# The up projection of a two-layer trunk's MLP by Strassen's seven products, with the tokens' operands made once a layer

## The chip, the core and the metric

The kernel runs on one core of one Trainium2 chip, with nothing on the other cores. Its metric is the device time of one execution in microseconds (us). Before the change three runs gave 2859.17 us (median), 2856.69 us (lowest) and 2861.38 us (highest).

## What is computed

1024 tokens of 1024 features pass a decoder trunk of two layers in float32: an HGRN2 mixer and an MLP, then latent attention (MLA) and a second MLP, then a last norm. The change lies in the two MLPs, which are alike:

```
def rmsnorm(x, gain):
    y = xf * lax.rsqrt(jnp.mean(xf * xf, axis=-1, keepdims=True) + EPS)
    return (y * gain).astype(x.dtype)

def sq_relu_mlp(xn, w_up, w_down):              # 1024 -> 4096 -> 1024 features
    return jnp.square(jax.nn.relu(xn @ w_up)) @ w_down

for l in range(DEPTH):
    h = h + mixer(rmsnorm(h, ...))              # HGRN2 for l = 0, MLA for l = 1
    h = h + sq_relu_mlp(rmsnorm(h, mlp_norm[l]), mlp_w_up[l], mlp_w_down[l])
return rmsnorm(h, final_norm)
```

## The kernel before

Features lie on the 128 partitions and tokens along the rows. The residual stream is two tiles `res` (the code's `hT[0]`, `hT[1]`), one for each half of 512 tokens, eight blocks of 128 features in each. Every product is made to nearly full float32 precision from three matmuls: an operand is split into a high part (a ScalarE cast) and a low part (the operand less its high part, on VectorE or GpSimd), and high x high, high x low and low x high are added up in PSUM (`mm3`, L92 to L98). A matmul here always moves 512 columns.

The stages follow each other: HGRN2 (0 to about 650 us), first MLP (to about 1350), MLA (to about 2165), second MLP (to about 2848), and the end.

An MLP of before begins with the norm. `inv_rms` squares eight blocks on ScalarE (L472), adds them on VectorE (L474), sums over the partitions with one matmul by ones (L476), and makes 1/rms by Ln, Exp and one Newton step (L478 to L480, L108 to L110). `fnorm` makes each normed block (L490) and `split` its parts (L90 on ScalarE, L91 on VectorE), 512 columns at a time, into the tiles `xn`. This is done for the first half of the tokens under a high priority, and for the second half between the first hidden features. Its temporary tiles come from a pool (`npers`, seven tiles) that all stages share.

Then come 4096 hidden features. `hidden` (L519) makes 128 of them for 512 tokens by 24 matmuls (L98) and squares the ReLU (L529, L530). The first and the last 256 of them go by `plain`: 96 matmuls up and 96 down, all L98. The other 3584 go by seven blocks of `fast`, 512 hidden features each: 192 matmuls up (L98), then the down product by Winograd's form of Strassen's scheme, seven products of 24 matmuls each (L613), over halves of the hidden features, of the outputs and of the tokens. Sums of weights are made on GpSimd and sums of hidden features on VectorE (L595), the parts by L600 and L601 (weights) and L90, L91 (`hh`, `hl`), with three buffers for each of `hh` and `hl`. Each product's four PSUM tiles are added to the stream by VectorE (L618).

A scheduler sets the order of each engine's instructions when the program is built, by program order and priority; at run time each engine works through its own list in order and waits on semaphores. A tile can be written only when whoever used that piece of memory before is through.

## Time and profile before

| | |
|---|---|
| median of 3 runs | 2859.17 us |
| span of the profiled execution | 2859.5 us |
| PE (TensorE matmul) busy | 2741.5 us, 96% |
| DVE (VectorE) busy | 1783.7 us, 62% |
| POOL (GpSimd) busy | 1054.6 us, 37% |
| ACT (ScalarE) busy | 896.9 us, 31% |
| matmuls L98 and L613 on the chain that ended last | 45% and 19% of the span |

Engine names in the profile: PE is TensorE's matmul, PEld its weight load, DVE is VectorE, ACT is ScalarE, POOL is GpSimd, SP is the queue that issues DMAs. The record of a matmul is longer (about 390 ns) than its share of the pipeline, so the cost of a matmul is read from the chain of waits, where a piece is a stretch of matmuls with its count. "a <- b" beside a wait names the instruction that ended it. PEclk is the granted TensorE clock as a share of full speed (2.4 GHz); 0.5 is its lower level (1.2 GHz).

### The profile page before, as it was taken

How to read it: one execution, taken by the hardware profiler on the slowest of the kernel's cores; microseconds unless marked ns; L12 is line 12 of the kernel's file. 1: busy time of each engine (PE TensorE's matmuls, PEld its weight loads, DVE VectorE, ACT ScalarE, POOL GpSimd, SP SyncE). 2: the span in 40 equal slices, each digit the busy share in tenths (PEclk: the TensorE clock that was granted, in tenths of full speed). 3: DMA queues.
4: the chain of work that ended last, by engine and by line, in shares of the span. 5: the costliest groups of instructions: out<-in, count | busy, mean ns of one | idle time of the engine just before them, and what ended most of it. 6: DMA issues, size and time to landing. Idle time of an engine off the chain costs nothing.

```text
span 2859.5 us, 34588 instructions
## 1 busy us (share of the span) xinstructions
PE 2741.5 (96%) x13573; PEld 2271.3 (79%) x13573; DVE 1783.7 (62%) x2924; ACT 896.9 (31%) x1672; POOL 1054.6 (37%) x584
## 2 busy tenths in 40 slices
PE   7999999898999999999889999999999999999998
PEld 5877777677888888887678888888887888888886
DVE  6667767766455566546676666676668455556555
ACT  4222233222222222222354444444445222222223
POOL 3222223343445455444321223122222455455443
PEclk9999999899999999999999999999999999999999
DMA  4111112133111111101211111111101111111102
GB/s 128 37 38 38 30 38 60 59 92 96 37 45 52 59 59 59 52 23 42 66 44 34 28 47 37 40 29 50 45 22 67 40 42 54 57 59 60 52 23 74
DMA packets 149665, 143.95 MB, mean 50 GB/s; under 512 B 11458, under 2 KB 122111, under 8 KB 149503
## 3 DMA queue, kind: packets, MB, share of 16 engines
q1 hardware_dynamic: 149502, 141.75, 16.4%
q8 instruction: 107, 1.75, 0.3%
q14 instruction: 56, 0.45, 0.1%
HBM read 133.33 MB, written 4.19 MB: 48 GB/s over the span
## 4 chain that ended last, share of the span: by engine, by line
PE 82%; DVE 12%; ACT 3%; issue 2%; DMA 0%; POOL 0%; SPq 0%; DVEq 0%; ACTq 0%; POOLq 0%
PE mm L98 45%; PE dn L613 19%; PE s L856 6%; PE nb L889 3%; PE mm L896 2%; PE x L356 2%; PE dn L98 2%; DVE xn L91 1%; DVE y L110 1%; ACT P L862 1%; DVE acc L474 1%; DVE t L109 1%; PE x L253 1%; DVE k L332 1%; DVE t L108 1%
## 5 line engine op out<-in xcount | busy, mean ns | idle before, releaser
L98 PE MATMUL mm<-xn,wh 128*128 128x512 f32 x3776 | 1206.2, 397 | 12.9 <-DVE res L435 8.0
L98 PEld LDWEIGHTS mm<-xn,wh 128*128 128x128 f32 x3776 | 708.2, 190 | 157.7 <-issue 11.0
L98 PE MATMUL mm<-xn,wl 128*128 128x512 f32 x1888 | 748.0, 396 | 0.0
L136 POOL TENSOR_TENSOR wl<-wst,wh 128x1024 fp32r<-128x1024 f32 (+2 forms) x165 | 394.9, 2396 | 250.0 <-ACT wh L133 241.6
L98 PEld LDWEIGHTS mm<-xn,wl 128*128 128x128 f32 x1888 | 358.0, 190 | 72.0 <-issue 1.1
L135 POOL TENSOR_SCALAR wh<-wst 128x1024 fp32r<-128x1024 f32 (+2 forms) x129 | 142.7, 1109 | 344.0 <-PE mm L98 218.9
L529 ACT ACTIVATE r<-mm 128x512 f32<-128x512 f32 x128 | 76.2, 595 | 582.2 <-PE mm L98 582.1
L618 DVE TENSOR_TENSOR res<-res,dn 128x512 f32<-128x512 f32 x308 | 201.5, 680 | 70.3 <-PE dn L613 69.1
L601 POOL TENSOR_TENSOR wl<-wa,wh 128x1024 fp32r<-128x1024 f32 x56 | 134.6, 2404 | 267.1 <-ACT wh L600 267.1
L865 POOL TENSOR_SCALAR P<-P,rc 128x128 f32<-128x128 f32 (+1 forms) x64 | 52.2, 815 | 347.9 <-DVE rc L863 333.5
L601 POOL TENSOR_TENSOR wl<-ws,wh 128x1024 fp32r<-128x1024 f32 x42 | 100.9, 2403 | 202.5 <-ACT wh L600 202.5
L613 PE MATMUL dn<-hh,wh 128*128 128x512 f32 x392 | 153.2, 391 | 0.0
L613 PE MATMUL dn<-wh,hh 128*128 128x512 f32 x392 | 153.2, 391 | 0.0
L613 PE MATMUL dn<-wh,hl 128*128 128x512 f32 x392 | 152.7, 389 | 0.0
L613 PE MATMUL dn<-hl,wh 128*128 128x512 f32 x392 | 152.7, 389 | 0.0
L613 PE MATMUL dn<-wl,hh 128*128 128x512 f32 x392 | 152.7, 389 | 0.0
L613 PE MATMUL dn<-hh,wl 128*128 128x512 f32 x392 | 152.7, 389 | 0.0
L530 DVE TENSOR_TENSOR fr<-r,mm 128x512 f32<-128x512 f32 x56 | 37.8, 685 | 175.8 <-ACT r L529 175.3
L530 DVE TENSOR_TENSOR res<-r,mm 128x512 f32<-128x512 f32 x56 | 37.8, 685 | 175.8 <-ACT r L529 175.4
L91 DVE TENSOR_TENSOR hl<-bs,hh 128x1024 fp32r<-128x1024 f32 x42 | 104.5, 2489 | 60.4 <-ACT hh L90 60.4
L862 ACT ACTIVATE P<-s,mx 128x384 f32<-128x384 f32 (+7 forms) x128 | 95.0, 743 | 138.0 <-DVE mx L860 118.2
L889 PE MATMUL nb<-h,xn 128*128 128x256 f32 (+1 forms) x640 | 136.7, 292 | 0.1
(253 smaller groups left out, 5213.2 us busy)
## 6 DMA issues: line engine op xcount, KB each, us to landing
wst<-mlp_w_up SPq DMA_DIRECT2D x64, 512.0 KB, 3.7
wa<-mlp_w_down SPq DMA_DIRECT2D x56, 512.0 KB, 3.8
wst<-hgrn_w_o SPq DMA_DIRECT2D x16, 512.0 KB, 3.7
wst<-mla_w_o SPq DMA_DIRECT2D x16, 512.0 KB, 3.7
wst<-hgrn_w_q SPq DMA_DIRECT2D x10, 512.0 KB, 3.8
wst<-hgrn_w_i SPq DMA_DIRECT2D x10, 512.0 KB, 3.7
wst<-hgrn_w_g SPq DMA_DIRECT2D x10, 512.0 KB, 3.7
wst<-hgrn_w_f SPq DMA_DIRECT2D x9, 512.0 KB, 3.7
```

Source lines behind the costliest of these rows:

```text
L91: V.tensor_tensor(out=out_l, in0=src, in1=out_h.bitcast(F32), op=ALU.subtract)
L98: T.matmul(ps, l, r, start=i == 0, stop=i == n - 1)
L135: G.tensor_scalar(out=wh[:, cs], in0=st[:, cs], scalar1=1.0, scalar2=1.0, op0=ALU.mult, op1=ALU.mult)
L136: G.tensor_tensor(out=wl[:, cs], in0=st[:, cs], in1=wh[:, cs].bitcast(F32), op=ALU.subtract)
L529: S.activation(out=r, in_=ps, func=AF.Relu)
L530: V.tensor_tensor(out=f, in0=r, in1=ps, op=ALU.mult)
L601: G.tensor_tensor(out=wl, in0=wa, in1=wh.bitcast(F32), op=ALU.subtract)
L613: T.matmul(banks[i], l, r, start=start and n == 0, stop=n == 5, skip_group_check=not start)
L618: V.tensor_tensor(out=o, in0=o, in1=banks[i], op=ALU.add)
L856: T.matmul(ps[:, at + u * HALF:at + u * HALF + w_], l, r, start=e == 0, stop=e == len(terms) - 1)
L862: S.activation(out=pt[:, :n], in_=sc, func=AF.Exp, bias=mx, accum_out=sm)
L889: T.matmul(dst, l, r[:, cols_], start=j == 0 and e == 0, stop=j == 2 * g + 1 and e == 2)
```

## The change

The up projection goes by the same seven-product scheme, for 256 hidden features at a time: over halves of the hidden features, of the input features and of the tokens. A product is 12 matmuls (L608), so 256 features take 84 matmuls; before they took four tiles of 24, which is 96. The down projection goes by `fast`'s scheme for all eight blocks of 512 features (`times`, L692; VectorE's add is L699), and `plain` is gone. In the whole program 13067 matmuls become 12635: 432 fewer, 216 in each layer (192 up, 24 down).

The token side of the up products are seven operands, made once a layer, each with a high and a low part: the two quarters B11, B21 and B22 of the normed tokens as they are, and the sums T1 to T4. `inverse` makes 1/rms for both halves of the tokens, with one tile each for the sum and the square; `normed` makes the normed quarters as float32 (L561); `rest` makes the second half, the sums (`combine`) and all remaining parts (`halves`, L567 and L525), 1024 columns at a time. `rest` stands behind the first two products in the first `up`. T1 needs the second half of the tokens; T2 and T3 need the sums too.

The temporary tiles of `inverse` are now the MLP stage's own tiles `hh` and `hl` (two buffers each, three before), and the pools for weights, norm and PSUM belong to a stage (`common`) instead of the whole program. Weights are loaded and split 512 columns at a time: five raw buffers, four pairs of parts.

```
-            NB = DFF // 256
-            def hidden(up, j, u, f):
-                mm3(ps, [(up[k // 4][0][:, k % 4, js], up[k // 4][1][:, k % 4, js], xh[:, k, :], xl[:, k, :])
-                         for k in range(KT)])
...
+            def inverse(u):
+                ta, tb = wide(tag="hh"), wide(F32, tag="hl")
+                acc, s, y, t = ta[:, 0], ta[:, 1], tb[:, 0], tb[:, 1]
+                for k in range(KT):
+                    sq = acc if k == 0 else s
+                    S.activation(out=sq, in_=hT[u][:, k, :], func=AF.Square)
+                    if k:
+                        V.tensor_tensor(out=acc, in0=acc, in1=sq, op=ALU.add)
+                ps = pbank()
+                T.matmul(ps, onef, acc, start=True, stop=True)
...
+            def halves(eng, key, src):
+                for k in (slice(0, 2), slice(2, 4)):
+                    S.copy(out=X[key][0][:, k], in_=src[:, k])
+                    sub(eng, X[key][1][:, k], src[:, k], X[key][0][:, k].bitcast(F32))
...
+            def rest():
+                normed(0, 1, y1)
+                combine(V, f[0, 1], f[0, 1], f[0, 0])
+                normed(1, 1, y1)
+                halves(G, "B22", f[1, 1])
+                combine(V, f[1, 1], f[1, 1], f[0, 1])
+                combine(V, f[0, 0], f[1, 1], f[0, 0])
+                halves(V, "T2", f[1, 1])
+                halves(V, "T1", f[0, 1])
+                halves(V, "T3", f[0, 0])
+                combine(G, f[1, 0], f[1, 0], f[1, 1])
+                halves(G, "T4", f[1, 0])
...
+            def up(A, C, between=None):
+                w11, w12 = parts(G, A[0, 0]), parts(V, A[0, 1])
+                sub(G, A[1, 0], A[1, 0], A[1, 1], ALU.add)
+                s1 = parts(V, A[1, 0])
+                product(x, w11, "B11", True, True)
+                product(y, w12, "B21", True, True)
+                if between is not None:
+                    between()
+                S.copy(out=C[0, 0], in_=x)
+                product(x, s2, "T2", False, True)
+                product(z, s1, "T1", True, True)
+                product(x, s3, "T3", False, True)
+                product(z, s4, "B22", False, True)
+                product(x, w22, "T4", False, True)
...
+            for fb in range(DFF // 512):
+                up(A, {...}, rest if fb == 0 else None)
+                up(nxt, {...})
+                down(down_A, last)
```

How the order of instructions moves, at three places. The first is ScalarE's list where HGRN2 ends and the first MLP begins. Before, the squares of the second half of the tokens (L472) stand between the copies (L434) that end HGRN2's output projection; those of the first half stand earlier still.

```order
293 L472 ACTIVATE s_5705<-res_5272 128x512
294 L434 COPY res_5272<-x_5466 128x512
295 L472 ACTIVATE s_5708<-res_5272 128x512
296 L434 COPY res_5272<-x_5506 128x512
297 L472 ACTIVATE s_5711<-res_5272 128x512
298 L434 COPY res_5272<-x_5546 128x512
299 L472 ACTIVATE s_5714<-res_5272 128x512
300 L434 COPY res_5272<-x_5586 128x512
301 L472 ACTIVATE s_5717<-res_5272 128x512
302 L478 ACTIVATE y_5722<-nb_5720,eps 128x512
```

After, the copies are L442 and the squares L547; `hh` holds the sum and the square, `wh` is a weight's high part.

```order
273 L442 COPY res_5272<-x_5506 128x512
274 L442 COPY res_5272<-x_5546 128x512
275 L547 ACTIVATE hh_5616<-res_4786 128x512 x2
276 L442 COPY res_5272<-x_5586 128x512
277 L547 ACTIVATE hh_5657<-res_5272 128x512
278 L547 ACTIVATE hh_5616<-res_4786 128x512
279 L547 ACTIVATE hh_5657<-res_5272 128x512
280 L598 CAST wh_5698<-wu_5682 128x512
281 L547 ACTIVATE hh_5616<-res_4786 128x512
282 L547 ACTIVATE hh_5657<-res_5272 128x512
283 L598 CAST wh_5702<-wu_5684 128x512
```

All but two of the sixteen squares now stand behind the last copy, which waits for PE's last transposes of HGRN2; the two halves of the tokens take turns, and casts of weights stand between them.

The second place is VectorE's list in the same stretch. Before, it makes the normed blocks (`f`, L490) and their low parts (`xn`, L91) in groups, with the end of HGRN2's output projection (L435) between them.

```order
987 L490 SCALAR_TENSOR_TENSOR f_5649<-res_4786,vecs,y_5628 128x512
988 L490 SCALAR_TENSOR_TENSOR f_5653<-res_4786,vecs,y_5628 128x512
989 L490 SCALAR_TENSOR_TENSOR f_5657<-res_4786,vecs,y_5628 128x512
990 L91 TENSOR_TENSOR xn_5602<-f_5649,xn_5601 128x512
991 L91 TENSOR_TENSOR xn_5602<-f_5653,xn_5601 128x512
992 L91 TENSOR_TENSOR xn_5602<-f_5657,xn_5601 128x512
993 L490 SCALAR_TENSOR_TENSOR f_5661<-res_4786,vecs,y_5628 128x512
994 L490 SCALAR_TENSOR_TENSOR f_5665<-res_4786,vecs,y_5628 128x512
995 L435 TENSOR_TENSOR res_5272<-res_5272,mm_5279 128x512
```

After, from the second half's normed quarters on (`xn_5605` and `xn_5607` are T1's and B22's high and low parts; the list is the whole of `rest` on VectorE):

```order
1006 L561 SCALAR_TENSOR_TENSOR fr<-res_5272,vecs,hl_5658 128x512 x4
1007 L525 TENSOR_TENSOR fr<-fr 128x1024 x2
1008 L561 SCALAR_TENSOR_TENSOR other<-res_5272,vecs,hl_5658 128x512 x4
1009 L525 TENSOR_TENSOR xn_5607<-fr,xn_5605 128x1024
1010 L525 TENSOR_TENSOR other<-other,fr 128x1024 x2
1011 L525 TENSOR_TENSOR fr<-other,fr 128x1024 x2
1012 L525 TENSOR_TENSOR T2l<-other,T2h 128x1024 x2
1013 L525 TENSOR_TENSOR xn_5607<-fr,xn_5605 128x1024
1014 L525 TENSOR_TENSOR T3l<-fr,T3h 128x1024 x2
```

The second half of T1's low part (the row before the last) stands behind both halves of T2's.

The third place is PE's list from HGRN2's last transposes (`x`) on. Before, the first hidden features follow at once, each matmul triple with 128 features of the first half of the tokens:

```order
2371 L433 MATMUL x_5586<-ident,xr_5584 128x128 x4
2372 L98 MATMUL mm_5732<-xn_5601,wh_5671 128x512
2373 L98 MATMUL mm_5732<-xn_5602,wh_5671 128x512
2374 L98 MATMUL mm_5732<-xn_5601,wl_5672 128x512
2375 L98 MATMUL mm_5732<-xn_5601,wh_5671 128x512
2376 L98 MATMUL mm_5732<-xn_5602,wh_5671 128x512
```

After, the two sums over the partitions (L551) come behind the transposes, then the products by B11, B21, T1 (`xn_5605`, `xn_5607`) and T2:

```order
2370 L441 MATMUL x_5586<-ident,xr_5584 128x128 x4
2371 L551 MATMUL ps_5633<-hh_5616,onef 128x512
2372 L551 MATMUL ps_5674<-hh_5657,onef 128x512
2373 L608 MATMUL ps_5711<-xn_5604,wh_5698 128x512 x4
2374 L608 MATMUL ps_5711<-xn_5606,wh_5698 128x512 x4
2375 L608 MATMUL ps_5711<-xn_5604,wl_5699 128x512 x4
2376 L608 MATMUL ps_5712<-xn_5604,wh_5702 128x512 x4
2377 L608 MATMUL ps_5712<-xn_5606,wh_5702 128x512 x4
2378 L608 MATMUL ps_5712<-xn_5604,wl_5703 128x512 x4
2379 L608 MATMUL ps_5713<-xn_5605,wh_5707 128x512 x4
2380 L608 MATMUL ps_5713<-xn_5607,wh_5707 128x512 x4
2381 L608 MATMUL ps_5713<-xn_5605,wl_5708 128x512 x2
```

Behind the transposes PE has the sums, 24 matmuls that need the first half of the tokens only, and then nothing that does not need `rest`. In the second MLP the lists are the same but for groups of four transposes of the stream (16 in all, some six of them among the products by T1 and T2).

## Rows read from the trace of the kernel before

**Rows 1.** The page's head, and its busy times.
```profile
span 2859.5 us, 34588 instructions
PE 2741.5 (96%) x13573; PEld 2271.3 (79%) x13573; DVE 1783.7 (62%) x2924; ACT 896.9 (31%) x1672; POOL 1054.6 (37%) x584
```

**Rows 2.** Chain that ended last, one block of 512: start, length (us), what.
```profile
734.12 43.52 PE mm L98 x192
777.64 38.18 PE dn L613 x168
```

**Rows 3.** PE's waits from 620 to 740: us, times, longest.
```profile
PE mm L98 <- DVE res L435: 7.7, 2, 7.4
PE nb L476 <- DVE acc L474: 1.1, 2, 0.6
```

**Rows 4.** Windows: length, PE, PEld, DVE, ACT, POOL busy (instructions), PEclk, DMA, GB/s.
```profile
648.40:656.00 7.60, 0.22 (x2) 0.24 (x2) 7.60 (x8) 3.18 (x6) 3.48 (x2) 0.71 0.43 123
656.00:662.00 6.00, 6.00 (x15) 4.68 (x16) 3.43 (x6) 2.01 (x4) 0.00 (x0) 0.52 0.01 3
2145.00:2233.30 88.30, 83.24 (x398) 67.24 (x397) 70.71 (x99) 36.39 (x66) 20.20 (x11) 0.96 0.20 66
2848.50:2859.50 11.00, 0.21 (x1) 0.00 (x0) 7.13 (x19) 4.03 (x12) 3.09 (x3) 0.71 0.51 191
```

**Rows 5.** Chain that ended last, the first MLP's norm.
```profile
630.28 0.64 ACT s L472
630.95 1.47 DVE acc L474
...
633.63 0.70 ACT y L478
...
638.04 4.10 DVE f L490 x3
...
653.72 1.32 DVE f L490 x2
655.04 0.61 DVE res L435
```

**Rows 6.** GpSimd's timeline beside that norm: start, length, engine, line, operation.
```profile
637.55 2.71 POOL L136 TENSOR_TENSOR wl<-wst,wh 128x1024 fp32r<-128x1024 f32 x1
...
649.31 2.65 POOL L136 TENSOR_TENSOR wl<-wst,wh 128x1024 fp32r<-128x1024 f32 x1
```

**Rows 7.** VectorE's timeline in a down product of the first MLP.
```profile
1091.23 2.58 DVE L91 TENSOR_TENSOR hl<-bs,hh 128x1024 fp32r<-128x1024 f32 x1 [4.32 <-ACT hh L90]
...
1095.04 1.22 DVE L595 TENSOR_TENSOR bs<-fr,bs 128x1024 f32<-128x1024 f32 x1
```

**Rows 8.** GpSimd's timeline in the same stretch.
```profile
1090.32 2.41 POOL L601 TENSOR_TENSOR wl<-ws,wh 128x1024 fp32r<-128x1024 f32 x1 [1.16 <-ACT wh L600]
```

**Rows 9.** Groups by line and form: busy us, mean ns; idle before, and its end.
```profile
L618 DVE TENSOR_TENSOR res<-res,dn 128x512 f32<-128x512 f32 x308 | 201.5, 680 | 70.3 <-PE dn L613 69.1
L316 POOL TENSOR_TENSOR pr<-q,k 128x512 f32<-128x512 f32 x16 | 21.1, 1317 | 123.7 <-DVE t L109 91.9 <-DVE q L284 20.6 <-DVE t L108 9.9
L90 ACT CAST hh<-bs 128x1024 fp32r<-128x1024 f32 x42 | 43.9, 1046 | 0.0
L90 ACT CAST xn<-f 128x512 fp32r<-128x512 f32 x40 | 24.5, 621 | 54.1 <-DVE f L490 38.6 <-PE mm L98 14.7
```

**Rows 10.** PE's waits from 2145 to 2240.
```profile
PE mm L98 <- DVE xn L91: 4.4, 3, 1.8
```

**Rows 11.** Chain that ended last, one group of four transposes in the second MLP.
```profile
2149.52 0.44 PE dn L977 x4
```

**Rows 12.** PE's waits from 1300 to 1500, where MLA begins.
```profile
PE nb L476 <- DVE acc L474: 8.7, 2, 4.6
PE dn L98 <- DVE res L565: 2.8, 2, 2.1
```

More of the change, by code (lines that the diff above doesn't have):

```diff
@@ new lines, in combine @@
+            def combine(eng, out, x, y):
+                for k in (slice(0, 2), slice(2, 4)):
+                    sub(eng, out[:, k], x[:, k], y[:, k])
+            with tc.high_priority(offset=1000):
+                y0 = inverse(0)
+                normed(0, 0, y0)
+                halves(V, "B11", f[0, 0])
+                normed(1, 0, y0)
+                halves(V, "B21", f[1, 0])
+            y1 = inverse(1)
+            def rest():
[10 more added lines that the diff above has]
+                halves(G, "T4", f[1, 0])
@@ new lines, in parts, with product @@
+            def parts(eng, x):
+                wh, wl = small("wh"), small("wl")
+                wh, wl = (t.rearrange("p (k c) -> p k c", k=x.shape[1]) if len(x.shape) == 3 else t for t in (wh, wl))
+                S.copy(out=wh, in_=x)
+                sub(eng, wl, x, wh.bitcast(F32))
+                return wh, wl
+            def product(bank, w, key, start, stop):
+                xh, xl = X[key]
+                terms = [(w[0], xh), (w[0], xl), (w[1], xh)]
+                n = 0
+                for l, r in terms:
+                    for k in range(4):
+                        T.matmul(bank, l[:, k, :], r[:, k, :], start=start and n == 0, stop=n == 11,
+                                 skip_group_check=not start)
+                        n += 1
@@ new lines, in weights, with hidden, times @@
+            def weights(A):
+                return [parts(G, A[:, k, :]) for k in range(2)]
+            def hidden(Bq):
+                hh, hl = wide(F32R, "hh"), wide(F32R, "hl")
+                S.copy(out=hh, in_=Bq)
+                sub(V, hl, Bq, hh.bitcast(F32))
+                return hh, hl
+            def times(banks, w, h, start, outs, ended=None):
+                hh, hl = h
+                if start:
+                    banks = [pbank() for _ in range(4)]
+                for k in range(2):
+                    wh, wl = w[k]
@@ L639, in mlp @@
-            for fb in range(1, NB - 1, 2):
-                fast(fb, fr)
-            plain(NB - 1)
+                        for n, (x, y) in enumerate(((wh, hh), (wh, hl), (wl, hh))):
+                            l, r = (x[:, si], y[:, k, :]) if finish is None else (y[:, k, si], x)
+                            T.matmul(banks[i], l, r, start=start and k == 0 and n == 0, stop=k == 1 and n == 2,
+                                     skip_group_check=not start)
+                        if k == 0:
+                            continue
@@ new lines, in mlp @@
+            stream = hT if finish is None else None
+            dn = other if finish is None else None
+            A = load_up(0)
+            for fb in range(DFF // 512):
+                last = fb == DFF // 512 - 1
+                nxt = load_up(2 * fb + 1)
+                up(A, {(i, u): B[:, u, i] for i in range(2) for u in range(2)}, rest if fb == 0 else None)
+                if fb == 0 and finish is not None:
+                    stream = finish.prepare(mp, pbank, other)
+                    dn = res_tile(1)
+                down_A = load_down(fb, dn)
+                A = None if last else load_up(2 * fb + 2)
+                up(nxt, {(i, u): B[:, 2 + u, i] for i in range(2) for u in range(2)})
+                down(down_A, last)
@@ L964, in build, with prepare @@
     class Finish:
[L965 to L968 removed]
+        def prepare(self, mp, pbank, first):
+            self.htok = []
             for u in range(2):
                 src = hT[u]
[L971 removed]
+                t = first if u == 0 else res_tile(0)
                 dst = t.rearrange("p (c d) -> p c d", c=4)
```

322 lines of the change are left out of this document (174 added, 148 removed).

## The prediction

> **What bounds the kernel now.** I read the page's busy times first, then the chain that ended last, then what PE waits for where the stages meet, and last the timelines of VectorE and GpSimd. PE is busy for 96% of the span, the next engine for 62% [rows 1]. Inside an MLP the chain is PE alone: 192 matmuls up in 43.52 us and 168 down in 38.18 us, which repeats for all seven blocks of each layer [rows 2]. So a matmul costs 0.227 us there, nothing else counts, and one fewer is worth as much. What PE loses lies at the seams: at the start of the first MLP it waits 7.7 us and 1.1 us [rows 3] and then runs six microseconds at its lower clock (PEclk 0.52) [rows 4]; at the start of the second MLP it waits 4.4 us [rows 10]. These waits are short because the norm is done beside the mixer's output projection: when PE has nothing left at 648.4, the first half's normed blocks are nearly made [rows 4, 5]. The question is what the change does to these two seams.
>
> **The matmuls.** 432 fewer at 0.227 us: -97.9 us, if PE stays the bound in the body of each MLP.
>
> **The body.** A block of 512 hidden features is now 336 matmuls, 76.3 us. In the up products a PSUM tile that is copied or added must be read before the next product but one goes into it; there lies a product of 12 matmuls (2.7 us) between, and the reader needs about 0.65 us. That costs nothing. In the down products there are two buffers of `hh` and `hl` instead of three, so the operand of a product is made only after the one two places ahead has ended: weights' casts and the operand's cast (two of 0.6 and one of 1.05 us [rows 9]), then VectorE's low part, 1.22 us alone and 2.58 us beside GpSimd [rows 7]. That is 3.5 to 4.9 us of a product's 5.4. VectorE also has four adds of 0.68 us [rows 9], which now come together in the second half of each product, because the PSUM tiles all end there, and once per block a sum of 1.22 us. Placed one after the other this just fits: when the adds of one product end, 0.6 us into the next, 2.8 us are left until the next adds. GpSimd's parts are now 512 wide (1.32 us for such an operation [rows 9]), so I take 1.5 us for the low part, with which the adds keep their place, and 2 us in all for hand-overs. With 2.58 us for low part and sum alike the second, fourth and fifth product are late by 1.5 us together: 24 us over 16 blocks. The bounds are 0 and 24.
>
> **The two starts.** This is the term that decides. The temporaries of the norm lie in the MLP's own tiles, and ScalarE's list has 14 of the 16 squares behind the copy that waits for PE's last transposes. I count from there (T0, which is 648.4 in the first MLP).
>
> (a) Squares and sums. For each half a square, an add, and the next square into the same tile: 0.64 + 0.69 and two hand-overs, 1.4 us (a square at 630.28, its add at 630.95 [rows 5]). Seven such steps are 10 us, with the two halves in turn. Between them GpSimd makes three sums and three low parts of weights, 1.32 us each. The trace shows what that does: `hl` starts at 1091.23 beside a GpSimd operation that began at 1090.32 and lasts 2.41; it ends 1.08 us after that one has ended, where alone it takes 1.22 [rows 7, 8]. So the two engines take turns when both read two SBUF operands, and five of the six GpSimd operations add 6.6 us. The last square of the second half stands ahead of the first half's Ln: 1.3 us. Ln starts at T0 + 18.
>
> (b) Ln, Exp and the Newton step to the first normed block: 633.63 to 638.04, 4.4 us [rows 5], and 0.6 for one operation of the other half between them: T0 + 23. The products by B11 and B21 follow as their parts come.
>
> (c) VectorE from there to T1's last low part, which ends PE's third product: 18 operations of 512 columns (16 normed blocks and two Newton operations) at 0.65 us, 11.7 us, and 14 of 1024 columns at 1.22 us, 17.1 us [rows 7]: 28.8 us alone. GpSimd in that time does three operations of 512 (4.0 us) and five of 1024 (2.41 us [rows 8], 12 us): 16 us. In full turns that is 44.8 us, to T0 + 68.
>
> How full are the turns? Before, VectorE's 15 operations of 512 from 638.04 to 655.65 took 17.6 us; at 0.61 (the last of them) they would take 9.2 [rows 5]. GpSimd had five operations there, the first at 637.55, the last at 649.31 [rows 6], 10 us together. 19 us in strict turns, 17.6 measured: nearly full. I take T0 + 65.
>
> The Trainium skill (SBUF — State Buffer, section "SBUF: two separate sides") calls the port pair of VectorE and GpSimd an exclusive lock: whichever starts first holds it for the whole instruction, and the other blocks. By that rule to the letter it is T0 + 68, and the sum below would be 6 us higher; by VectorE's own durations, without the rule, T0 + 46 and some 38 us lower. This case's rows stand close to the rule (17.6 of 19).
>
> (d) By then PE has done 30 matmuls (6.8 us of work), the products by B11 and B21 and half of T1's. After the wait it runs at the lower clock: 15 matmuls in 6.0 us instead of 3.4 [rows 4], 3 us with the edges. So the start costs 65 - 6.8 + 3 = 61 us, bounds 42 (no turns: (a) 11.3, (b) 5, (c) 28.8, and 1 us for hand-overs, in all T0 + 46) and 64.
>
> Before, the first start cost 7.7 + 1.1 + 2.6 = 11.4 us [rows 3, 4]: +49.6 us. In the second MLP some six groups of four transposes (0.44 us each [rows 11]) fill 2.6 us of the wait, and before PE was idle for 88.3 - 83.2 = 5.1 us [rows 4]: 61 - 2.6 - 5.1 = +53.3 us.
>
> **The other seams.** Where MLA begins, PE waits 8.7 us for the norm's sum and 2.8 us for the last adds [rows 12]. After, the sum over the partitions stands behind four matmuls of the first MLA product and waits for the same chain; the stage's tiles must wait for the MLP's. I take +1.5 us, bounds -3 and +5. At the end, 11 us lie between PE's last matmul and the end [rows 4]; now the last product's four tiles end 0.68 us apart and each asks for a square, an inverse root and a scaled write, where before they were spread. The last product also adds into PSUM tiles that VectorE must first have read. +2 us, bounds 0 and +4.
>
> **The sum.** -97.9 + 49.6 + 53.3 + 2 + 1.5 + 2 = +10.5 us on a span of 2859.5: 2870 us. The span is within 0.4 us of the median of the runs, 2859.17, so that is my forecast: 2870 us, slower by 0.4%. A change of less than 0.2%, about 5.7 us, is what a measurement of this kernel can't tell from none. With the starts between 57 and 64 and the body between 0 and 10 us this case spans 2857 to 2886.
>
> **Rivals.**
>
> (1) GpSimd hardly slows VectorE in the starts, because its operations fall into ScalarE's gaps. For it: VectorE has gaps while squares are made. Against it: from the first normed block on VectorE's list has no gap to fall into. Starts of 42 to 46 us: -97.9 + 32.6 + 36.3 + 5.5 (from 44) = -23.5 us, 2836 us, faster. It decides when the 14 operations of 1024 columns take below about 1.8 us on the mean.
>
> (2) The norm stays hidden behind the mixer as before, and all of the 98 us is saved: 2761 us. For it: the squares' inputs are there early, in the first half well before T0. Against it: ScalarE's list, where they stand behind the last transposes' copy.
>
> (3) The down products become VectorE's: low parts and sums of 1024 take 2.58 us there as they did before, and every block is late by 1.5 us. +22 us on the forecast, 2892 us. It decides when the mean of `hl` is above 2.2 us. For it: 2.58 in a row of before. Against it: GpSimd's operations beside it are half as long and come before ScalarE's cast of the operand is through.
>
> **Chances.** My own case 0.52, rival (1) 0.31, (2) 0.03, (3) 0.14. My own case gives faster 0.03, the same 0.16, slower 0.33; rival (1) reaches the same with 0.02, the rest is faster; (2) is faster; (3) is slower but for 0.01. That is faster 0.03 + 0.29 + 0.03 = 0.35, the same 0.19, slower 0.33 + 0.13 = 0.46. The range leaves out rival (2) and the far end of (1) and (3): 2828 to 2894.
>
> **What will show it.** Each step has its place in the profile after. The body: up and down pieces of 168 and 168 matmuls of 38.1 us in the chain of waits, repeated 16 times without VectorE between them; if it is wrong, PE's waits on the adds (L699) or on the low parts of `hh` appear 14 times or more. The starts: PE's first product by B11 20 to 27 us after the last transposes, and full pace 60 to 70 us after them; the longest waits on low parts (L525) of T1. The turns: low parts of 1024 columns beside GpSimd at 2 us or more in `rest`. If full pace comes 45 us after T0, rival (1) holds; if it comes in 10 us, (2).
>
> What would make the prediction wrong most easily: a start shorter than 55 us, since both starts are alike and each microsecond counts twice.

## The result and the profile after

The changed kernel takes 2929.62 us (median of four runs, 2924.12 to 2931.26); the kernel before, run beside it, 2857.93 us. The ratio is 1.0248, 95% interval 1.0233 to 1.0263: slower by 2.5%. The forecast was slower by 0.4%, 2870 us; the time lies outside its range (2828 to 2894). The direction was right, the size was not.

The page after, its head and its busy times, against [rows 1]:

```profile
span 2927.7 us, 35228 instructions
PE 2674.8 (91%) x13141; PEld 2196.7 (75%) x13141; DVE 1853.0 (63%) x2954; ACT 1200.1 (41%) x2240; POOL 1368.2 (47%) x874
```

PE has 67 us less to do and waits in places where it did not. GpSimd is busy for 314 us more, VectorE for only 69. PE's waits over the whole span (us in total, times, longest; `...` marks rows left out, here and below):

```profile
PE ps L551 <- DVE hh L549: 32.7, 2, 16.6
PE ps L608 <- DVE xn L525: 30.7, 7, 17.5
PE ps L608 <- ACT xn L567: 21.7, 7, 5.5
PE ps L608 <- ACT fr L634: 20.5, 15, 1.5
PE nb L484 <- DVE acc L482: 18.3, 2, 14.2
...
PE ps L692 <- DVE hl L525: 10.0, 18, 1.2
```

The first three are the two starts. The fourth and the last come once in nearly every block of 512. The fifth is where MLA begins. The spans of the two profiled runs are 68.2 us apart (the medians 71.7). Lined up by events that both traces have, these 68.2 us are, to 0.4 us: matmuls -97.9; an earlier end of HGRN2's core -3.1; first start +49.7; second start +50.2; the bodies of the two MLPs +34.0; where MLA begins +20.7; inside MLA +2.0; the end +12.2. (The expectations below speak of 30 us for the bodies, from a first reading that had put the last 12 up matmuls of each MLP on the wrong side of the mark.)

The first start, from the chain that ended last (start, length, what):

```profile
673.65 0.45 PE x L441 x4
...
700.82 3.09 PE ps L608 x6
...
722.66 4.43 DVE other L525 x2
727.09 6.57 DVE fr L525 x2
...
741.42 15.29 PE ps L608 x56
```

PE runs on without a wait ("full pace") 67.3 us after the last transposes (674.1). In the second MLP, counted from the end of MLA's output projection (2210.7), it is 67.4. What stretches it shows in the timelines of GpSimd and of VectorE, one below the other:

```profile
726.03 6.54 POOL L525 TENSOR_TENSOR other<-other 128x1024 f32<-128x1024 f32 x2 [1.16 <-DVE other L525]
732.53 6.62 POOL L525 TENSOR_TENSOR T4l<-other,T4h 128x1024 fp32r<-128x1024 f32 x2
```

```profile
727.01 6.65 DVE L525 TENSOR_TENSOR fr<-other,fr 128x1024 f32<-128x1024 f32 x2
733.58 6.65 DVE L525 TENSOR_TENSOR T2l<-other,T2h 128x1024 fp32r<-128x1024 f32 x2
740.15 1.21 DVE L525 TENSOR_TENSOR xn<-fr,xn 128x1024 fp32r<-128x1024 f32 x1
```

Each pair lasts 6.6 us on both engines; once GpSimd is through, the same form takes VectorE 1.21 us. One instruction of each engine takes 3.3 us for both, where the two last 1.21 and 2.40 alone, 3.6 together: they go by turns.

One block of 512 in the body, from the chain again. Before it was two pieces of PE alone [rows 2]:

```profile
873.25 21.83 PE ps L692 x95
895.08 19.05 PE ps L608 x84
...
914.17 1.29 POOL wu L525
915.47 1.26 POOL wl L525
...
916.79 2.16 POOL wu L525
...
918.98 0.62 ACT wh L598
919.60 0.95 ACT hh L677
920.54 0.49 ACT fr L634
...
921.08 13.91 PE ps L608 x60
...
935.13 2.09 POOL wl L525
...
937.29 3.28 POOL other L525
...
940.59 1.14 ACT wh L598 x2
941.74 0.97 ACT hh L677
...
942.73 2.21 DVE hl L525
...
944.96 2.20 DVE fr L525
947.16 2.39 DVE res L699 x4
949.55 2.35 DVE hl L525
```

The next block begins at 951.94: 78.7 us for 336 matmuls that need 76.2. The chain leaves PE twice. The first time ScalarE's copy of a PSUM tile (L634) stands in its list behind a weight's cast that waits for a GpSimd sum; the second time the hidden's cast (`hh`) stands behind two such casts, and VectorE's low part, sum, four adds and low part follow. Of its eight GpSimd and VectorE pieces with two SBUF operands, six are longer than they are alone (1.21 on VectorE; 1.3 and 2.40 on GpSimd for 512 and 1024 columns). An estimate from these rows: with the durations that they have alone, the second stretch would be 4.8 us shorter, far more than PE waits there; the first only 0.9, where PE waits 1.5.

### The profile page after: what moved, and what is told of

It reads as the page before. It is cut to its first block, busy times and chain, and to the rows that moved or that the text cites. A ratio compares the mean times of both kernels' runs of the same rounds, so it can differ in the third digit from the quotient of the medians.

```text
span 2927.7 us, 35228 instructions
## 1 busy us (share of the span) xinstructions
PE 2674.8 (91%) x13141; PEld 2196.7 (75%) x13141; DVE 1853.0 (63%) x2954; ACT 1200.1 (41%) x2240; POOL 1368.2 (47%) x874
## 4 chain that ended last, share of the span: by engine, by line
PE 66%; DVE 19%; ACT 6%; POOL 6%; issue 3%; DMA 1%; SPq 0%; DVEq 0%; POOLq 0%; ACTq 0%
PE mm L106 21%; PE ps L608 17%; PE ps L692 12%; PE s L986 5%; PE nb L1019 3%; DVE hl L525 3%; POOL wu L525 2%; PE mm L1026 2%; DVE fr L525 2%; PE x L364 2%; POOL wl L525 2%; DVE res L699 1%; ACT wh L598 1%; ACT hh L677 1%; DVE xn L99 1%
## 5 line engine op out<-in xcount | busy, mean ns | idle before, releaser
L106 PE MATMUL mm<-xn,wh 128*128 128x512 f32 x1728 | 570.2, 404 | 1.6 <-DVE xn L228 1.0
L106 PEld LDWEIGHTS mm<-xn,wh 128*128 128x128 f32 x1728 | 322.8, 191 | 64.8 <-issue 3.5
L106 PE MATMUL mm<-xn,wl 128*128 128x512 f32 x864 | 349.0, 404 | 0.0
L144 POOL TENSOR_TENSOR wl<-wst,wh 128x1024 fp32r<-128x1024 f32 (+1 forms) x93 | 221.1, 2380 | 243.4 <-ACT wh L141 240.5
L608 PE MATMUL ps<-xn,wh 128*128 128x512 f32 x1024 | 265.1, 400 | 52.7 <-DVE xn L525 30.7
L525 POOL TENSOR_TENSOR wl<-wu,wh 128x512 fp32r<-128x512 f32 x160 | 216.5, 1357 | 175.6 <-ACT wh L598 99.1
L608 PEld LDWEIGHTS ps<-xn,wh 128*128 128x128 f32 x1024 | 193.9, 192 | 104.3 <-DVE xn L525 35.3
L525 POOL TENSOR_TENSOR wu<-wu,wu 128x512 f32<-128x512 f32 x128 | 182.5, 1426 | 163.4 <-DVE wl L525 126.4
L525 DVE TENSOR_TENSOR hl<-fr,hh 128x1024 fp32r<-128x1024 f32 x110 | 196.6, 1789 | 88.9 <-ACT hh L677 88.9
L699 DVE TENSOR_TENSOR res<-res,ps 128x512 f32<-128x512 f32 x352 | 229.9, 682 | 16.1 <-PE ps L692 15.3
L525 POOL TENSOR_TENSOR wl<-other,wh 128x512 fp32r<-128x512 f32 x112 | 173.1, 1557 | 57.5 <-ACT wh L598 53.3
L525 POOL TENSOR_TENSOR wl<-res,wh 128x512 fp32r<-128x512 f32 x112 | 172.6, 1553 | 54.1 <-ACT wh L598 50.1
L106 PEld LDWEIGHTS mm<-xn,wl 128*128 128x128 f32 x864 | 165.2, 191 | 32.8 <-issue 1.6
L692 PE MATMUL ps<-wh,hl 128*128 128x512 f32 x448 | 176.3, 394 | 7.4 <-DVE hl L525 5.1
L692 PE MATMUL ps<-hh,wh 128*128 128x512 f32 x448 | 176.0, 393 | 6.6 <-DVE res L699 6.6
L692 PE MATMUL ps<-hl,wh 128*128 128x512 f32 x448 | 176.7, 395 | 5.1 <-DVE hl L525 4.9
L692 PE MATMUL ps<-wh,hh 128*128 128x512 f32 x448 | 175.2, 391 | 1.4 <-DVE res L699 1.4
L692 PE MATMUL ps<-hh,wl 128*128 128x512 f32 x448 | 175.7, 392 | 0.0
L692 PE MATMUL ps<-wl,hh 128*128 128x512 f32 x448 | 174.8, 390 | 0.0
L525 DVE TENSOR_TENSOR fr<-fr 128x1024 f32<-128x1024 f32 x62 | 117.9, 1904 | 71.9 <-ACT fr L613 70.9
```

Of the source, the lines that this page charges most:

```text
L106: T.matmul(ps, l, r, start=i == 0, stop=i == n - 1)
L144: G.tensor_tensor(out=wl[:, cs], in0=st[:, cs], in1=wh[:, cs].bitcast(F32), op=ALU.subtract)
L525: eng.tensor_tensor(out=out, in0=x, in1=y, op=op)
L608: T.matmul(bank, l[:, k, :], r[:, k, :], start=start and n == 0, stop=n == 11, skip_group_check=not start)
L692: T.matmul(banks[i], l, r, start=start and k == 0 and n == 0, stop=k == 1 and n == 2, skip_group_check=not start)
L699: V.tensor_tensor(out=o, in0=o, in1=banks[i], op=ALU.add)
```

## Experiments

All times are medians beside runs of the kernel before on the same chip; the number is this one's, the interval that of its ratio. "The changed kernel" is 2929.6 us.

### The copies

```diff
-                S.copy(out=C[0, 0], in_=x)
+                V.tensor_copy(out=C[0, 0], in_=x)
```

> Change: in each up step the copy of the first product's PSUM tile is made by VectorE instead of ScalarE, nothing else. In the changed kernel's trace a block of 512 lasts 78.6 us where 336 matmuls would take 76.2; PE waits up to 1.9 us a block for this copy, which stands in ScalarE's list behind a weight's cast that waits for GpSimd and behind a cast of 1024. Theory A (the loss in the body is ScalarE's list): about 1.4 us a block are gained in 15 blocks, the time falls by 16 to 24 us, to about 2909 us, and PE's waits for the copy are gone. Theory B (the loss is the turns of VectorE and GpSimd, so that the weights' parts come late anyway): the next wait, for the weights' parts, takes its place, and the time stays within 6 us of 2929.

2925.27 us, ratio 1.0216 to 1.0247: theory B's time, but the wait moved to the other copy (L639: 15.1 us, 13 times) and not to the weights' parts. Then both copies, C[0, 0] and C[0, 1]:

> Change: in each up step both copies of the first PSUM tile (after the first product and after the product by T2) are made by VectorE instead of ScalarE. With the first copy alone moved the time fell by 4 us only, and PE waited 15.1 us in 13 places for the second copy, on ScalarE. Theory A (ScalarE's list is jammed there by two casts of 1024 for the down operands and a weight's cast that waits for GpSimd, and any copy on it is late): both waits go, 1.4 us in each of 15 blocks, the time falls by 16 to 24 us against the changed kernel, to about 2909 us. Theory B (what is late there is the weights' parts): the wait moves on to a weight's part, and the time stays at 2922 to 2930 us.

2927.22 us, 1.0228 to 1.0258. PE no longer waits for copies, but in the same four blocks (873 to 1188) for the down product's low parts. The changed kernel first, then this one:

```profile
PE ps L608 <- ACT fr L634: 6.1, 4, 1.5
```

```profile
PE ps L692 <- DVE hl L525: 7.5, 8, 1.2
```

A block still lasts 78.6 us. So the copy is where the loss shows, not where it is made.

### The starts: the tokens' operands off GpSimd, and a plain first step

```diff
-                halves(G, "B22", f[1, 1])
+                halves(V, "B22", f[1, 1])
-                combine(G, f[1, 0], f[1, 0], f[1, 1])
-                halves(G, "T4", f[1, 0])
+                combine(V, f[1, 0], f[1, 0], f[1, 1])
+                halves(V, "T4", f[1, 0])
```

> Change: at the start of each MLP, B22's low part, T4's sum and T4's low part are made by VectorE instead of GpSimd (the last two behind T3 in VectorE's list). VectorE gets two more operations of 1024 ahead of T1's last low part, GpSimd loses five there. Theory A (VectorE and GpSimd take turns, nearly in full): GpSimd's 12 us go, 2.3 us come, so full pace comes some 8 to 10 us earlier after the last transposes (67.4 us before), in both layers: 16 to 20 us less, about 2912 us. Theory B (they don't hold each other up there, VectorE's list is long by itself): full pace comes 2 to 5 us later in each layer, about 2936 us.

2904.86 us, 1.0148 to 1.0182: theory A, with more than its 20 us. VectorE has six operations of 1024 more to do, two of them ahead of T1's last low part, and full pace comes 56.7 us after the last transposes in place of 67.3. The pair of sums that took 6.65 us beside GpSimd takes 2.35 without it:

```profile
720.84 2.35 DVE L525 TENSOR_TENSOR fr<-other,fr 128x1024 f32<-128x1024 f32 x2
```

The results that GpSimd made here are not on the way to T1, so it is the turns that lengthened the starts. On top of it, the first 256 hidden features of a layer by 96 plain matmuls (no T is needed), with the sums made beside them:

```diff
-                up(A, {...}, rest if fb == 0 else None)
+                (plain if fb == 0 else up)(A, {...})
```

> Change: on top of the kernel with the rest on VectorE (2904.9 us), the first 256 hidden features of each layer go by plain products: 96 matmuls instead of 84, on the four quarters B11, B21, B12, B22 (B12's parts lie in T4's tiles until then), and the sums T1 to T4 are made beside them. Theory A (a start costs what VectorE's chain lasts beyond the work that PE has for it): PE gets 96 matmuls, 21.8 us, instead of 30 before it must wait for sums, at the price of 12 matmuls, 2.7 us, a layer; VectorE's list is 4.6 us longer for B12's low part. 10 to 18 us a layer are gained, about 2876 us. Theory B (VectorE's list is the bound anyway, since its end sets when the second up step gets T2 and T3): the gain is eaten by the longer list and the 2.7 us, the time is within 6 us of 2905.

2893.75 us, 1.0111 to 1.0145: another 11 us (theory A had 20 to 36).

### The norm made in the stage before

The first half's norm moved into HGRN2's and MLA's output projections, with four raw weight buffers in place of five to make room.

> Change: the norm of the first half of the tokens and its parts (B11, B21) are made with temporaries of the stage before, in the mixer's stage, as the kernel before did; 1/rms is kept, and the normed quarters are made a second time for the sums. Six norm temporaries instead of seven and four raw weight buffers instead of five make room for it. Theory A (each start is the serial chain from the last transposes on, and what is taken out of it is gained): 8 squares, 8 of the 16 weighted adds, 8 normed blocks and four low parts of 1024 leave the chain; full pace comes 15 to 25 us earlier in both layers (67.4 us after the last transposes before), the time falls by 30 to 50 us, to about 2890 us. Theory B (the chain is set by the second half of the tokens and GpSimd's turns, the first half runs beside it): under 10 us a layer, 2915 us or more.

2934.57 us, 1.0255 to 1.0285. Full pace came 56.2 us after the last transposes, 11 sooner, but those came 14 us later: PE waited for the stream within the output projection (7.7 us, longest 7.4) as before the change [rows 3]. A block lasted 79.2 us; that there were four raw buffers and not five may be why, but this was not tried by itself. Nothing won.

### Where MLA begins

```diff
-                down(down_A, last)
+                down(down_A, last and finish is not None)
```

> Change: the last block of the first MLP's down projection takes its seven products in the order of the other blocks (w5, w1, w3, w6, w7, w4, w2) instead of its own (w1, w2, w6, w7, w4, w5, w3). From the last up step's end to a mark in MLA the changed kernel lost 23.5 us more than the kernel before. Theory A (VectorE is full there: 28 adds, 7 low parts and sums of 1024 columns, and MLA's 16 low parts and 14 adds, in whatever order): the place of the loss moves, 25 us of PE's idle time stay within 5 us, the time within 6 us of 2929. Theory B (the order is the cause: it asks for the last up step's result in its second product, which is why PE waits at once): the waits at the block's start go, some 6 to 10 us, and the time falls by that.

2917.93 us, 1.0196 to 1.0226. The wait for the norm's sum (L482) falls from 18.3 to 10.0 us. The last block of the first MLP has an order of its own in the changed kernel; with the other blocks' order 11.7 us come back. The other suspect was VectorE's load of low parts there, 16 of which went to GpSimd:

```diff
+                    G.tensor_tensor(out=xl[:, k, :], in0=hT[u][:, k, :], in1=xh[:, k, :].bitcast(F32), op=ALU.subtract)
```

> Change: where MLA begins, the 16 low parts of the stream (512 columns) are made by GpSimd instead of VectorE, nothing else. After the last up step of the first MLP the changed kernel's VectorE is busy for 95% of 76 us, and PE waits 18.3 us for the norm's sums. Theory A (VectorE is full there): 16 operations of 0.6 us and their turns, 10 to 16 us, leave VectorE's list; the norm's sums come 8 to 12 us earlier, about 2919 us. Theory B (the order of the last block's outputs sets it, and GpSimd, which folds MLA's weights then, makes the low parts later than VectorE did): no gain or a loss, 2928 us or more.

2929.24 us, 1.0234 to 1.0264. No gain: the wait for the sum stays (18.8) and a GpSimd operation is waited for instead (7.6).

### All four together

Both copies and the tokens' operands on VectorE, the plain first step, and the last block's order.

> Change: all at once: rest on VectorE, both copies on VectorE, first 256 hidden features plain, the first MLP's last block in the order of the others. If the four losses are separate, the gains add up: 2929.6 - 25 - 20 - 12 - 28 = 2845 us, under the kernel before (2857.8). If VectorE, which takes all the work moved here, becomes the bound at the starts and in the up steps, it is 2870 us or more.

2889.14 us, 1.0093 to 1.0125, not the 2845 of gains that add up. The body still lost 2.4 us a block, and the first start showed a new wait of 13.0 us, for a single GpSimd instruction:

```profile
712.87 22.79 POOL L525 TENSOR_TENSOR wl<-wu,wh 128x512 fp32r<-128x512 f32 x1 [26.16 <-ACT wh L603]
735.62 1.27 POOL L525 TENSOR_TENSOR wu<-wu,wu 128x512 f32<-128x512 f32 x1
```

The next one of this size takes 1.27 us. From 712.8 to 734.5 VectorE worked through 20 operations of two SBUF operands without a gap, at their own pace (1.17 us for 1024 columns); GpSimd's ended 1.1 us after that list had its first pause. This was the hint for the body.

### The body: whose list sets it?

```diff
-                return [parts(G, A[:, k, :]) for k in range(2)]
+                return [parts((G, V)[k], A[:, k, :]) for k in range(2)]
```

> The changed kernel with the low part of the second half of each of down's seven weight operands made on VectorE in place of GpSimd (7 of 14 per block of 512). A block lasts 78.6 us in the changed kernel, its 336 matmuls 76.2. Theory A, GpSimd's list sets the block: in the down part ScalarE waits 4.31 us for GpSimd's sum at 937.29, and the hidden's cast stands behind it. Seven low parts of 1.3 to 1.4 us taken from that list are some 9 us, four times the 2.4 us lost: a block falls to 76.2 to 76.6, fifteen blocks and a half in all make -25 to -30 us, 2900 to 2905. Theory B, VectorE's own last series (hl 2.20, fr 2.20, four adds 2.47, hl 2.41) sets the block: seven operations of about 0.7 us more on VectorE make it longer, 2930 to 2945.

2919.07 us, 1.0196 to 1.0226. The wait for `hl` is gone, the copy's 1.5 us stays (4.6 us in three blocks). Less than half of what theory A said, but far from B: seven operations more on VectorE made the block shorter (78.0).

The four sums of `down` on VectorE:

```diff
-                    sub(G, A21, A21, A22, ALU.add)
+                    sub(V, A21, A21, A22, ALU.add)
```

> The changed kernel with down's four sums of weights per block (128x1024, 2.40 to 3.28 us each on GpSimd) on VectorE (2.20 us each there). Theory A, GpSimd's list sets the block: 10 to 11 us go from it, a block falls to 76.2 to 76.8, 2900 to 2910. Theory B, VectorE's list: 8.8 us more on it in the down part, where it is busy 20 of 26 us already: slower than 2930, up to 2990.

2926.79 us, 1.0221 to 1.0251. Neither theory's number: 2.8 us less than the changed kernel, which the two intervals do not tell from none. The copy's wait stays (6.1 us in four blocks).

The hidden's rounding:

```diff
-                S.copy(out=hh, in_=Bq)
+                V.tensor_copy(out=hh, in_=Bq)
```

> The changed kernel with the hidden's rounding (128x1024, 1.0 us on ScalarE, seven per block) on VectorE, so that the hidden no longer stands behind the weights' casts in ScalarE's list, and GpSimd's list is as it was. Theory A1, GpSimd is late only through the cast behind it in ScalarE's list: hl at 942.73 would start up to 3 us earlier, a block falls to 76.2 to 77, 2900 to 2915. Theory A2, GpSimd's list itself is late for the weights' low parts: the wait moves to wl, 2925 to 2935. Theory B, VectorE's list: seven casts of 1 to 2 us more on it, slower than 2935.

2957.2 us, 1.0327 to 1.0361: theory B. The cast on VectorE lasts 1515 ns on the mean, and the low parts are as long as in the changed kernel (1812):

```profile
L525 DVE TENSOR_TENSOR hl<-fr,hh 128x1024 fp32r<-128x1024 f32 x28 | 50.4, 1812 | 0.7
L677 DVE CAST hh<-fr 128x1024 fp32r<-128x1024 f32 x28 | 42.1, 1515 | 0.1
```

So VectorE's list matters, and yet giving it GpSimd's work helped. That fits neither A nor B alone; it fits if GpSimd's work was in part on VectorE's time already (theory C, below). Three runs on top of all four edits, with half of `down`'s low parts on VectorE first:

> The run of all four edits (2889.14) with half of down's low parts on VectorE as well. There a block waits 1.0 to 1.2 us twice for the hidden's low part, with both copies already on VectorE; half of the low parts by itself left only the copy's 1.5 us per block. Theory A, GpSimd's list in the down part makes that wait: both waits are gone, a block falls from 78.6 to 76.2, fifteen blocks in two layers' 16 make some -30 us: about 2860. Theory B, VectorE's list: the copies and the low parts together on VectorE keep the wait, 2880 or more.

2868.55 us, 1.0022 to 1.0045: 21 us less, near theory A's 2860.

All of `down`'s weight work, `parts(V, ...)` and `sub(V, ...)`, but for the four sums of the second MLP's last block:

> The run of all four edits with all 14 low parts and the four sums of down on VectorE: GpSimd has no work in the down part. Theory C, an operation of two operands on VectorE lasts longer while GpSimd works (128x1024: 1.21 us alone in the first start, 1.78 to 2.2 in a block, 3.36 beside GpSimd's sums in the start): the hidden's low parts fall to 1.2 to 1.3 us, 11 operations save some 10 us, which pays for most of the 14 of 0.68 and 4 of 1.2 that are added (14.3 us): the block stays at 76.2 to 77, 2855 to 2870. Theory B, VectorE's list in the down part is full (20 of 26 us busy): a block grows by 3 us and more, 2900 to 2960.

2845.53 us, 0.9947 to 0.9975, faster than theory C's range. In four blocks (873 to 1188) PE now waits for nothing, with GpSimd still at work in the up steps; the 13.0 us wait of the first start is still there.

And the weight work of `up` too:

> The run of all four edits with every low part and sum of the MLP's weights on VectorE, none on GpSimd. In the run of all four a low part of GpSimd, 1.3 us else, lasted 22.79 us in the first start while VectorE worked through its list without a gap, and TensorE waited 13.0 for it. Theory C (contention): that wait is gone, a block's operations last what they last alone, VectorE's sum of a block is some 65 us of 76: 2835 to 2860. Theory B (VectorE's list too long, its operations late for TensorE in the up part too): a block grows, 2900 to 3000.

2828.80 us, 0.9882 to 0.9911: 1.0% faster than the kernel before, the fastest of all, and again faster than theory C's range. The 13.0 us wait is gone, which is most of this step's 16.7. Each step that takes more from GpSimd is faster: theory C's direction, with more than its size.

### The one edit alone, and three controls

The changed kernel with only GpSimd's MLP work moved (every `parts(G, ...)`, `sub(G, ...)`, `halves(G, ...)` and `combine(G, ...)` of the MLP to `V`):

> The changed kernel with all of the MLP's work of GpSimd on VectorE (the tokens' operands, the weights' sums and low parts) and nothing else: the copies stay on ScalarE, the last block's order and the start with seven products as in the changed kernel. Theory C, the stretching of both engines' operations sets the block and part of the starts: the tokens' operands alone gave 25 us back, the body has 30 more: 2929.6 - 25 - 30 = 2875, range 2865 to 2882. Theory D, the copies on ScalarE make a wait of their own, as they did where half of down's low parts were taken away (1.5 us a block left): 22 of the 30 stay lost, 2890 to 2900.

2846.82 us, 0.9948 to 0.9974: 82.8 us less than the changed kernel, by who does the work alone, and 0.4% faster than before. It is more than theory C's 55, so stretching as I had priced it is not the whole of the gain. Windows of one block (length, PE, PEld, DVE, ACT, POOL busy), the changed kernel and this one:

```profile
873.25:951.94 78.69, 76.75 (x336) 62.91 (x336) 44.54 (x50) 36.20 (x59) 56.33 (x37) 1.00 0.17 54
```

```profile
873.25:951.94 78.69, 78.69 (x349) 65.16 (x348) 64.33 (x88) 38.23 (x60) 0.00 (x0) 1.00 0.18 57
```

In place of GpSimd's 56.3 us VectorE is busy for 19.8 us more. PE is busy without a gap, 349 matmuls in the time of 336, and over four blocks it waits for nothing. VectorE's groups by form in that block (busy us, mean ns), the changed kernel first:

```profile
L525 DVE TENSOR_TENSOR hl<-fr,hh 128x1024 fp32r<-128x1024 f32 x7 | 12.5, 1781 | 5.9 <-ACT hh L677 5.9
L525 DVE TENSOR_TENSOR fr<-fr 128x1024 f32<-128x1024 f32 x4 | 8.0, 1992 | 4.7 <-ACT fr L613 4.6
```

```profile
L525 DVE TENSOR_TENSOR wl<-other,wh 128x512 fp32r<-128x512 f32 x14 | 9.3, 686 | 0.1
L525 DVE TENSOR_TENSOR hl<-fr,hh 128x1024 fp32r<-128x1024 f32 x7 | 8.5, 1221 | 0.5 <-ACT hh L677 0.5
L525 DVE TENSOR_TENSOR fr<-fr 128x1024 f32<-128x1024 f32 x4 | 4.9, 1223 | 0.8 <-ACT fr L613 0.8
```

The hidden features' low parts and sums lose 7.1 us of stretching (12.5 and 8.0 become 8.5 and 4.9); the larger part of the difference between 56.3 and 19.8 is that VectorE is the faster engine for this work: 0.69 us for a low part of 512 columns (`wl`), which takes GpSimd 1.3 alone. So the move did two things at once, it ended the turns and it made the weights' parts come sooner, and for the body no run here parts the two.

Where the gain comes from, between the same events of both traces (the spans of the profiled runs are 80.4 us apart): 35.6 from HGRN2's last transposes to the first MLP's last up step, 8.7 from the first MLP's last product to MLA's last scores, 34.4 from there to the second MLP's last up step, and 4.0 after it; the first MLP's last down step is 3.1 longer. Of the 35.6, 17.6 are the wait for T1 (49.7 us after the transposes, not 67.3, with 30 matmuls done by then in both); the 18.0 left are seven and a half blocks of 2.4.

The copies back on ScalarE in the fastest version:

> The fastest version so far (2828.80) with both copies back on ScalarE. Theory C: without GpSimd no chain holds ScalarE's list, VectorE (65 of 78 us busy) is relieved of four operations of 0.69 us in a block: 2822 to 2831. Theory D, the copies on ScalarE stand behind the weights' casts and make TensorE wait 1.5 us in a block: some 20 us are lost, 2845 to 2855.

2831.38 us, 0.989 to 0.9923, and no wait in four blocks (873 to 1188). The copies were no cause of their own.

The one edit with the last block's order:

> The changed kernel with all of the MLP's GpSimd work on VectorE (2846.82) and the last block of the first layer in the other blocks' order. With it, the first 256 in plain form and the copies on ScalarE the time was 2831.38; the order alone gave 11.7 in the changed kernel. If order and engine add up: 2835, and the plain first 256 gives 4; if the wait that the other order removes is made by GpSimd's stretching as well: 2843 to 2848, and the plain first 256 gives the 15.

2844.19 us, 0.9931 to 0.9964: the order gives 2.6 and not 11.7 (the intervals do not tell 2.6 from none), so most of what it gave was also GpSimd's doing; the plain start gives the other 13 to the run above.

Last, the same move in the kernel before, where 60 weight casts of GpSimd went to ScalarE besides:

> The kernel before, with all of its MLP's GpSimd work on VectorE (the weights' low parts and sums; the 60 weight casts of GpSimd on ScalarE). Theory C says that the two engines stretch each other's operations, which costs time only where TensorE waits for them; in the body of the kernel before it waits for nothing (an empty row of waits over two blocks), so only the starts and the ends can gain: 2845 to 2860. Theory E, the gain is one of GpSimd's slowness that any MLP of this shape shows: as much as in the changed kernel, 2780 to 2800. Theory B, VectorE's list is too full: slower than 2870.

2855.11 us, 0.9979 to 0.9997: 0.1% less, under the 0.2% below which the prediction can't tell a change of this kernel from none. Its low parts were as stretched, and became as short; before, then with all on VectorE (800 to 1200):

```profile
L91 DVE TENSOR_TENSOR hl<-fr,hh 128x1024 fp32r<-128x1024 f32 x20 | 38.8, 1960 | 1.8 <-ACT hh L90 1.8
L91 DVE TENSOR_TENSOR hl<-bs,hh 128x1024 fp32r<-128x1024 f32 x14 | 34.9, 2491 | 21.6 <-ACT hh L90 21.6
```

```profile
L91 DVE TENSOR_TENSOR hl<-fr,hh 128x1024 fp32r<-128x1024 f32 x20 | 24.0, 1219 | 0.0
L91 DVE TENSOR_TENSOR hl<-bs,hh 128x1024 fp32r<-128x1024 f32 x14 | 17.1, 1221 | 0.0
```

The stretching was there before the change and cost nothing: PE waits for nothing in these 400 us of either run. Why the same stretching costs time after it is argued and not shown: 43.5 us of up products in each block gave slack [rows 2], and GpSimd was busy for 201.7 of the 400 us; in the block after it is busy for 56.3 of 78.7, with its sums and low parts for the up products on top.

## Why the prediction was wrong, step by step

**The matmuls** (-97.9; the traces hold 432 fewer) and **the starts** were right. The first cost +49.7 (forecast +49.6), the second +50.2 (+53.3). That the first agrees to a tenth is luck: full pace came at T0 + 67.3, not 65, and the first start of before had lost some 2 us more than the 11.4 that I counted (13.7 from 628 to 720, by its matmuls at 0.227 us). The Trainium skill (SBUF — State Buffer, section "SBUF: two separate sides") says that whichever of the two engines starts first holds the shared ports for its whole instruction. By that I had T0 + 68, and the trace comes near it, though not by my count: six GpSimd operations of 1024 lie in that stretch and not five, so strict turns would be T0 + 70. Rival (1), that GpSimd hardly slows VectorE in the starts, is refuted by the run with the tokens' operands on VectorE: more operations on VectorE, and full pace 10.6 us sooner. One reading was wrong without harm: 648.4 before was a gap within HGRN2's output projection and not its end; its last transposes end at 688.5, so HGRN2 lasts to there and not to 650.

**The body** failed, at the step "Placed one after the other this just fits", with "2 us in all for hand-overs" (bounds 0 to 24; measured 34.0). I took 1.5 us for a low part; they last 1.78 on the mean, and the sums 1.99 where I had 1.22, and there are four of them in a block, not one. But longer VectorE operations are not all of it: 2.58 us for each was to cost 24 us, and the loss is 34 at less. The step placed VectorE's list alone and put GpSimd's own list at nothing, which is busy for 56.3 us of a block's 78.7. The copy that "costs nothing" stands in ScalarE's list behind a cast that waits for a GpSimd sum, and so does the hidden's cast. So the wait was not one engine's but went round through all four, and the edits to the copies moved it on. Taking GpSimd's work away ended it; how much of the 34 was the turns and how much GpSimd's own length stays open. Rival (3) named a part of the mechanism with the wrong threshold: it was to decide above a mean of 2.2 us, and the loss came at 1.78. I had counted turns for the starts and taken 1.5 us in the body, although [rows 7] had the 2.58.

**Where MLA begins** (forecast 1.5, bounds -3 to 5; measured 20.7) was mis-sized: no term of the sum held the last block's own order. I looked at the norm's sum and not at what the last block's own order leaves to VectorE just there: from 1365 to 1396 it is busy 28.7 of 31 us, with GpSimd busy 25.1 beside it:

```profile
1365.00:1396.00 31.00, 13.05 (x42) 8.94 (x41) 28.66 (x26) 9.57 (x17) 25.06 (x13) 0.76 0.21 56
```

The order took 11.7 of it; with all on VectorE the order is worth 2.6. PE's wait for the sum goes from 18.3 to 10.5 and, with both, to 6.7 us.

**The end** (2, bounds 0 to 4; measured 12.2) was mis-sized as well. PE's last matmul ends 14.2 us before the end in place of 11 [rows 4], and its last 168 matmuls take 8.6 us longer than 168 in the body: 5.7 of waits (after 2860) and some 3 more, part of it at a lower granted clock (0.77 on the mean from 2906 to 2913.5), while VectorE is busy for 25 of the last 32 us:

```profile
PE ps L692 <- DVE f_v L1135: 2.3, 1, 2.3
PE ps L692 <- DVE hl L525: 2.0, 2, 1.2
PE ps L692 <- DVE res L699: 1.4, 2, 1.1
```

```profile
2895.90:2927.70 31.80, 15.07 (x57) 11.44 (x56) 25.11 (x62) 16.62 (x49) 12.06 (x9) 0.78 0.35 132
```

The adds, squares and scaled writes come all at once there, as I had said, but I had not worked out their price. Four microseconds go with GpSimd's work; the rest was not tried by itself and stays open.

The body's +32, MLA's +19 and the end's +10 over the forecast, less 6 for the second start and HGRN2's end, with 2 in MLA, are the 57 us by which the sum was short of the spans' difference.

## What to carry to other kernels

A duration in a trace is its price in that neighbourhood: when a change takes slack from the bounding engine, look whether VectorE's and GpSimd's two-operand instructions last longer together than alone, and price every list with the longer figure, GpSimd's own list too. When a wait moves from place to place as single edits are made, the cause is not at the place where it shows; change who does the work for a whole class of operations at once. Work given to GpSimd is not free for VectorE: here 56.3 us of it a block, taken back, added only 19.8 to VectorE's list, since VectorE does it in about half the time and 7 us of stretching ended.

## What the hardware showed

Two-operand float32 instructions of VectorE and GpSimd on SBUF go by turns: 1.21 us becomes 3.3 us beside GpSimd's 128x1024 operations in the start, and 1.78 to 2.49 on the mean in the bodies. The Trainium skill (Perfetto Trace Analysis, section "Optimizing Scalar/DVE Operations") says that moving work between these two might not help, since they share a read port; here, back on VectorE, it gave 82.8 us. The turns are not fair, either: the record of one GpSimd instruction, 1.27 us else, lasts 22.79 us, over 20 of VectorE's that keep their own pace, while in other stretches the same two engines took turns. By the Trainium skill (SBUF — State Buffer, section "SBUF: two separate sides") whichever starts first holds the ports for its whole instruction, and the other blocks. A GpSimd instruction that waits for one of VectorE's would by that end within 2.5 us (an estimate: 1.17 and 1.27); it took 22.79, and the measurement decides. What makes the one case or the other these runs don't show.
